# Turning q and k of each head on VectorE and by DMAs between partitions instead of on TensorE, in a two-layer trunk

## The chip, the cores and the metric

The kernel runs on one core of one Trainium2 chip. The time is device microseconds of one execution of the whole program. The engines in question are TensorE (PE in the rows; PEld are its weight loads), VectorE (DVE), ScalarE (ACT), GpSimd (POOL) and SyncE (SP); SP and POOL issue the DMAs here.

## What is computed

The program is a trunk of two layers on 512 tokens of width 2048, in f32. Each layer normalizes, scales and shifts by rows that come from a conditioning vector c, mixes the tokens, and adds the gated result to the residual. Layer 0 mixes by causal pooling, layer 1 by sparse attention with 16 heads of 128, where a small indexer picks the allowed keys of every query. Cut to what matters:

```python
def rms_norm(x, g):
    return x * lax.rsqrt(jnp.mean(x * x, axis=-1, keepdims=True) + EPS) * g

# layer 1 (dsa_branch); layer 0 is pool_branch
q, k, v, gate, qi, ki, wi = jnp.split(h @ w_in, ATTN_SPLITS, axis=-1)
q = rope_partial(q.reshape(B, L, 16, 128), positions, 32)
k = rope_partial(k.reshape(B, L, 16, 128), positions, 32)
score = einsum('bqhs,bqh->bqs', relu(einsum('bqhd,bsd->bqhs', qi, ki)), wi) * idx_scale
_, sel = lax.top_k(where(causal, score, -inf), 128)
logits = einsum('bqhd,bqkhd->bhqk', q, k[sel]) * 128 ** -0.5
o = einsum('bhqk,bqkhd->bqhd', softmax(logits), v[sel])
out = (o * silu(gate)) @ w_out
# each layer
h = rms_norm(x, norm_g[i]) * (1 + scale) + shift
x = x + gate_i * out
```

The logits contract over the head's 128 dimensions, so q and k must stand with these on the partitions, while the projection leaves them with tokens on the partitions: each needs a 512x128 transpose per head.

## The kernel before

Every f32 product is made of three matmuls on fp32r pairs: an operand is split into a high half (ScalarE, L174) and a low half, the rest (VectorE, L175), and high x high, high x low and low x high are summed. The program goes through these stages: sums of squares of x and the first norm; layer 0's projections, pooling and output; the second norm; the indexer and the choice of keys; q, k, v and the heads; layer 1's output; the final norm.

In the heads' stage the heads go in pairs j = 0..7 of an even head a and an odd head b. The projection of a pair is computed by seven products of half-size blocks, in the order P1, P5, P6, P3, P7, P2, P4. Each product has four units (kp), each unit 12 matmuls of 128x384 (q_slot, L812 to L814), into the PSUM tiles bx, by and bz. A unit's weights arrive in tiles qx or qy: one load (L734) on SP's queue, and for most products a second, accumulating load (L737) on POOL's. `q_unit` splits them into qwh and qwl three units ahead (QLOOK), four slots each; as P4's units are split, the load of the next pair's P1 goes out on SP. nb, the q, k, v of head b, is complete when P7's results are added (L951, two adds), na after P4's.

What a head then needs is a list of 13 items (head_items). They are queued in bg, and step(1) after each unit runs one of them, so the work of b stands in the program among P2, P4 and the next P1, that of a among the next pair's P1, P5, P6 and P3. The items are: rope of q and k (L541 to L544); the halves of v; `turned` for q and then for k, which makes four transposes of 128x128 into a PSUM tile (L835) and splits it into qh, ql or kh, kl; `soft` for each of four query blocks (three matmuls of 128 rows and 128 to 512 columns, L859 to L861, a masked maximum on VectorE, exp on ScalarE); norm_p; trans (transposes of the probabilities, L879); and pvs. The logits stand in tiles lg, a ring of three; the same ring serves s3_item and y_split.

A norm (norm_r) makes the reciprocal of mean square plus EPS, its root on ScalarE, and one Newton step in four GpSimd operations (L277 to L280); norm_b then turns the result into a row with TensorE (L286). At the start SP issues the row c (cr), the table of columns (cl), the first 1 MB of modulation weights (ms) for the scale, and then the 16 tiles of x; mod_scale and mod_shift are each a product of ms with silu(c), summed on VectorE (L226).

The order within an engine is settled when the program is built; at run time an instruction waits for semaphores. DMAs on SP and ACT share eight completion semaphores (DMAHW0 to 7), those on POOL eight others (DMASW0 to 7).

Of the kernel before, what the change touches and what calls it, by code (L numbers as in the profile page):

```python
# [52 lines left out]
def trunk(ctx, tc, xT, cols, crow, pos, modT, win, wgrp, wout0, widx, wgate, wqkv, wout1, out):  # L53
    nc = tc.nc
    mm = nc.tensor.matmul

    cp = ctx.enter_context(tc.tile_pool(name="cp", bufs=1))
    hp = ctx.enter_context(tc.tile_pool(name="hp", bufs=1))
    dp = ctx.enter_context(tc.tile_pool(name="dp", bufs=1, space=DRAM))
    P = {}  # L60
# [18 lines left out]
    turn = [0]  # L79
# [4 lines left out]
    def att():  # L84
        return P["ps"].tile([128, 512], F32, name="att", tag="att", bufs=P["natt"])
# [170 lines left out]
    def cond_rows(pool, rows):
        cr = rows()
        nc.sync.dma_start(cr, crow)
        cb = pool.tile([128, D], F32, name="cb")
        for q in range(4):  # L260
            p = bank()
            mm(p, ones[0:1, :], cr[:, 512 * q:512 * q + 512], start=True, stop=True)
            nc.scalar.activation(cb[:, 512 * q:512 * q + 512], p, AF.Silu)
        cell["cb"] = cb


    def norm_r(t0, t1):
        nb = (t1 - t0) // 128
        p = misc()
        for j in range(nb):  # L270
            mm(p[:, j:j + 1], P["acc"][:, t0 + j * 128:t0 + j * 128 + 128], ones[:, 0:1], start=True, stop=True)
        s = P["tp"].tile([128, 4, 4], F32, name="nrm", tag="nrm", bufs=2)
        v, r, u, iv = (s[:, a, 0:nb] for a in range(4))
        nc.vector.tensor_scalar(v, p[:, 0:nb], 1.0 / D, EPS, op0=OP.mult, op1=OP.add)
        nc.vector.reciprocal(iv, v)
        nc.scalar.activation(r, iv, AF.Sqrt)
        nc.gpsimd.tensor_tensor(u, r, r, op=OP.mult)  # L277
        nc.gpsimd.tensor_tensor(u, u, v, op=OP.mult)
        nc.gpsimd.tensor_scalar(u, u, -0.5, 1.5, op0=OP.mult, op1=OP.add)
        nc.gpsimd.tensor_tensor(r, r, u, op=OP.mult)  # L280
        return r

    def norm_b(r, t0, t1):
        p2 = misc()
        for j in range((t1 - t0) // 128):
            nc.tensor.transpose(p2[:, j * 128:j * 128 + 128], r[:, j:j + 1].to_broadcast([128, 128]), ident)  # L286
        nc.scalar.copy(P["rbc"][:, t0:t1], p2[:, 0:t1 - t0])

# [34 lines left out]
    em = ExitStack()  # L323
    ml = em.enter_context(tc.tile_pool(name="ml", bufs=1))

    cond_rows(ml, lambda: ml.tile([1, D], F32, name="cr", tag="ms", bufs=3))
    nc.sync.dma_start(cl, cols)
    for i in range(2):
        nc.vector.tensor_scalar(b1[:, i, :], mb_[:, 48 * i + 16:48 * i + 32], 1.0, None, op0=OP.add)
    mod_scale(ml, 0, 0)()  # L330
    acc2 = hp.tile([128, T], F32, name="acc2", tag="lo0")
    xs = []
    for k in range(KT):
        x_t = hp.tile([128, T], F32, name=f"x{k}", tag=f"hi{k}")
        nc.sync.dma_start(x_t, xT[k])
        add_square(x_t, 0, T, k < 2, lambda: hp.tile([128, T], F32, name=f"sq{k}", tag=f"lo{k}"),
                   to=(P["acc"], acc2)[k % 2])
        xs.append(x_t)
    nc.vector.tensor_tensor(P["acc"], P["acc"], acc2, op=OP.add)
    mod_shift(ml, 0, 0)()  # L340
    prefetch(1)
    norm_b(norm_r(0, T), 0, T)

    def mk(k):
        return lambda: (make_h(0, k, xs[k], 0, T), done.add(("h", k)))
# [187 lines left out]

    (cosa, sina), (cosi, sini) = rot["a"], rot["i"]

    def rope(pool, tag, x, cs, sn, shape, h):
        bc = lambda t: t[:, :, None, :].to_broadcast(shape[:3] + [t.shape[-1]])
        nel = shape[1] * shape[2]
        t1 = pool.tile([128, nel, 2 * h], F32, name="rt1", tag=tag + "1").rearrange("p (a b) c -> p a b c", a=shape[1])
        t2 = pool.tile([128, nel, 2 * h], F32, name="rt2", tag=tag + "2").rearrange("p (a b) c -> p a b c", a=shape[1])  # L540
        nc.vector.tensor_tensor(t1, x, bc(cs), op=OP.mult)  # L541
        nc.vector.tensor_tensor(t2[:, :, :, 0:h], x[:, :, :, h:2 * h], bc(sn[:, :, 0:h]), op=OP.mult)
        nc.vector.tensor_tensor(t2[:, :, :, h:2 * h], x[:, :, :, 0:h], bc(sn[:, :, h:2 * h]), op=OP.mult)
        nc.vector.tensor_tensor(x, t1, t2, op=OP.add)  # L544
# [24 lines left out]
    for tt, o in early:  # L569
        n = o.shape[-1]  # L570
# [20 lines left out]
    for c, tts in ((0, (2, 3)), (1, (1, 2, 3)), (2, (1, 2, 3))):  # L591
# [9 lines left out]
        else:  # L601
            a, n = ((0, 10), (10, 6))[c - 1]
# [179 lines left out]
    ap = el.enter_context(tc.tile_pool(name="ap", bufs=1, reuse_waits="tile"))  # L782
# [33 lines left out]

    def s3_item(k):
        def run():
            ha = ap.tile([128, T], F32, name="lg", tag="lg", bufs=3)
# [8 lines left out]
    def head_items(h, nat):  # L828
        x = nat.rearrange("p t (o d) -> p t o d", o=3)
        cell = {}  # L830

        def turned(s, nm):
            p = att()
            for tt in range(4):
                nc.tensor.transpose(p[:, tt * 128:tt * 128 + 128], x[:, tt, s, :], ident)  # L835
            a = ap.tile([128, T], F32R, name=nm + "h", tag=nm + "h")
            b = ap.tile([128, T], F32R, name=nm + "l", tag=nm + "l")
            split(a, b, p)
            cell[nm] = (a, b)

        def rot_qk():
            rope(ap, "rh", x[:, :, 0:2, 0:32], cosa, sina, [128, 4, 2, 32], 16)

        def keep_v():
            vh = ap.tile([128, 4, 128], F32R, name="vh", tag="vh")
# [8 lines left out]
        def soft(qb):  # L854
            n = (qb + 1) * 128
            (qh, ql), (kh, kl) = cell["q"], cell["k"]
            o = att()[:, 0:n]
            qs = slice(qb * 128, qb * 128 + 128)
            mm(o, qh[:, qs], kh[:, 0:n], start=True, stop=False)  # L859
            mm(o, qh[:, qs], kl[:, 0:n], start=False, stop=False)  # L860
            mm(o, ql[:, qs], kh[:, 0:n], start=False, stop=True)  # L861
            lg = ap.tile([128, n], F32, name="lg", tag="lg", bufs=3)
# [50 lines left out]
    def y_split(k):  # L913
        src = y[k]
        if k < HEADS - 2:
            src = ap.tile([128, T], F32, name="yr", tag="lg", bufs=3)
            nc.sync.dma_start(src, yd[k])
        yT[k] = hslots(k)
        split(yT[k][0], yT[k][1], src)

    ev = nc.vector.tensor_tensor
    for j in range(HEADS // 2):
        a, b = 2 * j, 2 * j + 1
        banks = {}
        na = nb = None
        for u in range(28):
# [4 lines left out]
            if role[prod] not in banks:  # L931
                r = role[prod]
# [46 lines left out]
    op_ = es.enter_context(tc.tile_pool(name="op", bufs=1))  # L979
# [97 lines left out]
```

## Time and profile before

| what | value |
|---|---|
| median of 3 runs | 1656.59 us (1652.77 to 1659.31) |
| the profiled execution | 1654.79 us, span 1653.0 us |
| TensorE busy | 1616.7 us, 98% of the span |
| VectorE, ScalarE, GpSimd busy | 1258.4, 726.2, 135.8 us |
| heads' stage | about 930 to 1447 us; one pair takes 70.50 us |

The span is the time from the first to the last instruction of the profiled execution; its own time is a little longer. A share is an average over stages: TensorE waits mainly in the first 32 us and the last 20.

### The profile page before, as it was taken

To read this page: it belongs to the slowest core of one execution; us is meant where nothing else is said; L and a number is where in the kernel's file an instruction comes from. 1 tells how busy PE (TensorE), PEld (TensorE's weight loads), DVE (VectorE), ACT (ScalarE), POOL (GpSimd) and SP (SyncE) were. 2 spreads that over 40 slices of the span, in tenths; PEclk is the share of its full clock that TensorE was granted. 3 is DMA by queue.
4 is the path that set the end of the run, shared out by engine and by line. 5 is a ranking of instruction groups with operands and counts; after the bars stand their busy time and mean duration, and the time that the engine had idled before them with its cause. 6 is when DMAs were issued, how large, how long until landed. Compare 5 with 4: busy or idle time off the path is not lost.

```text
span 1653.0 us, 23832 instructions
## 1 busy us (share of the span) xinstructions
PE 1616.7 (98%) x8892; PEld 1460.8 (88%) x8892; DVE 1258.4 (76%) x2132; ACT 726.2 (44%) x1149; POOL 135.8 (8%) x258
## 2 busy tenths in 40 slices
PE   4999999999999999999999999999999999999997
PEld 2888888888889999998889999999999999988897
DVE  6899998999974689865796676676776777756854
ACT  4622221334223456453324555455545555544244
POOL 1000000000000000010002121121312213000000
PEclk9999999999999999999999999999999999999999
DMA  8888888552786786443347896886968778637954
GB/s 323 326 299 310 325 337 327 223 178 101 286 300 208 233 249 187 143 143 114 102 149 169 197 174 164 185 165 177 165 170 178 171 180 162 205 109 288 364 175 166
DMA packets 105381, 348.21 MB, mean 211 GB/s; under 512 B 11825, under 2 KB 20145, under 8 KB 92849
## 3 DMA queue, kind: packets, MB, share of 16 engines
q1 hardware_dynamic: 86834, 296.35, 51.2%
q0 software_dynamic: 18432, 50.34, 18.2%
q8 instruction: 70, 1.15, 0.3%
q14 instruction: 45, 0.37, 0.1%
HBM read 330.39 MB, written 16.25 MB: 210 GB/s over the span
## 4 chain that ended last, share of the span: by engine, by line
PE 72%; issue 24%; POOL 1%; DVE 1%; DMA 1%; ACT 0%; POOLq 0%; SPq 0%; DVEq 0%; ACTq 0%
PE acc L191 8%; PE acc L192 8%; PE acc L193 8%; PE att L191 4%; PE att L192 4%; PE att L193 4%; PE by L812 4%; PE by L814 4%; PE by L813 4%; PE bz L812 2%; PE bz L814 2%; PE bx L812 2%; PE bz L813 2%; PE bx L814 2%; PE bx L813 2%
## 5 line engine op out<-in xcount | busy, mean ns | idle before, releaser
L148 ACT CAST wh<-st 128x1024 fp32r<-128x1024 f32 (+1 forms) x232 | 236.1, 1018 | 497.9 <-PE acc L192 267.3
L150 DVE TENSOR_TENSOR wl<-st,wh 128x1024 fp32r<-128x1024 f32 (+1 forms) x232 | 274.0, 1181 | 149.8 <-ACT wh L148 147.1
L192 PE MATMUL acc<-lo,wh 128*128 128x512 f32 (+1 forms) x810 | 299.7, 370 | 0.0
L191 PE MATMUL acc<-hi,wh 128*128 128x512 f32 (+1 forms) x810 | 299.6, 371 | 0.0
L193 PE MATMUL acc<-hi,wl 128*128 128x512 f32 (+1 forms) x810 | 299.2, 370 | 0.0
L226 DVE SCALAR_TENSOR_TENSOR ms<-ms,cb 128x2048 f32<-128x2048 f32 x96 | 218.9, 2285 | 17.4 <-DMA ms<-modT 8.8
L192 PEld LDWEIGHTS acc<-lo,wh 128*128 128x128 f32 x810 | 153.1, 189 | 26.4 <-DVE lo L175 0.2
L191 PEld LDWEIGHTS acc<-hi,wh 128*128 128x128 f32 x810 | 153.0, 189 | 26.5 <-ACT hi L174 0.4
L193 PEld LDWEIGHTS acc<-hi,wl 128*128 128x128 f32 x810 | 153.1, 189 | 26.2
L175 DVE TENSOR_TENSOR qwl<-qx,qwh 128x768 fp32r<-128x768 f32 x128 | 122.1, 956 | 67.1 <-ACT qwh L174 64.6
L174 ACT CAST qwh<-qx 128x768 fp32r<-128x768 f32 x128 | 106.7, 836 | 103.4 <-PE bz L814 37.3
L191 PE MATMUL att<-hi,wh 128*128 128x512 f32 (+1 forms) x406 | 148.8, 367 | 2.2 <-ACT hi L312 2.2
L192 PE MATMUL att<-lo,wh 128*128 128x512 f32 (+1 forms) x406 | 149.1, 367 | 0.0
L193 PE MATMUL att<-hi,wl 128*128 128x512 f32 (+1 forms) x406 | 148.9, 367 | 0.0
L175 DVE TENSOR_TENSOR qwl<-qy,qwh 128x768 fp32r<-128x768 f32 x96 | 91.7, 956 | 48.9 <-ACT qwh L174 47.0
L737 POOL DMA_DIRECT2D qx<-wqkv x96 | 83.3, 873 | 432.1 <-DVE stt L866 199.6
L174 ACT CAST qwh<-qy 128x768 fp32r<-128x768 f32 x96 | 80.0, 834 | 87.0 <-PE by L814 39.5
L191 PEld LDWEIGHTS att<-hi,wh 128*128 128x128 f32 x406 | 77.1, 190 | 14.9 <-ACT hi L312 2.6
L812 PE MATMUL bx<-qwh,hi 128*128 128x384 f32 x256 | 89.2, 349 | 0.0
L192 PEld LDWEIGHTS att<-lo,wh 128*128 128x128 f32 x406 | 77.1, 190 | 13.2 <-DVE lo L313 0.8
L193 PEld LDWEIGHTS att<-hi,wl 128*128 128x128 f32 x406 | 77.2, 190 | 12.5
L812 PE MATMUL by<-qwh,hi 128*128 128x384 f32 x256 | 88.2, 345 | 0.0
(286 smaller groups left out, 3507.2 us busy)
## 6 DMA issues: line engine op xcount, KB each, us to landing
ms<-modT SPq DMA_DIRECT2D x96, 1024.0 KB, 7.2
st<-wout SPq DMA_DIRECT2D x88, 512.0 KB, 4.4
qx<-wqkv POOLq DMA_DIRECT2D x96, 384.0 KB, 5.7
st<-win SPq DMA_DIRECT2D x64, 512.0 KB, 5.1
qy<-wqkv SPq DMA_DIRECT2D x64, 384.0 KB, 3.5
st<-wgate SPq DMA_DIRECT2D x40, 512.0 KB, 3.6
qx<-wqkv SPq DMA_DIRECT2D x32, 384.0 KB, 3.2
qy<-wqkv POOLq DMA_DIRECT2D x32, 384.0 KB, 5.9
```

What stands on the lines that cost most here:

```text
L148: nc.scalar.copy(wh, st)
L150: nc.vector.tensor_tensor(wl, st, wh.bitcast(F32), op=OP.subtract)
L174: nc.scalar.copy(hi, src)
L175: nc.vector.tensor_tensor(lo, src, hi.bitcast(F32), op=OP.subtract)
L191: mm(o, wh[:, kk, ms], rh[:, t0:t1], start=first, stop=False)
L192: mm(o, wh[:, kk, ms], rl[:, t0:t1], start=False, stop=False)
L193: mm(o, wl[:, kk, ms], rh[:, t0:t1], start=False, stop=last)
L226: nc.vector.scalar_tensor_tensor(st, st, 1.0, cell["cb"], op0=OP.mult, op1=OP.mult, accum_out=dst)
L737: nc.gpsimd.dma_start(d[kp], blk(j, name, kp), accum_op=OP.add)
L812: mm(o, hi, wh[:, kk, :], start=first, stop=False, skip_group_check=not opens)
L813: mm(o, hi, wl[:, kk, :], start=False, stop=False, skip_group_check=not opens)
L814: mm(o, lo, wh[:, kk, :], start=False, stop=last, skip_group_check=not opens)
```

## The change

The heads: `turn` takes the place of `turned`. Four VectorE instructions transpose every 32x32 block of a head's q (128 tokens each) into a tile b; 16 DMAs on SP's queue, each 32 partitions of 512 bytes (16 KB), then put block row i and block column j of b where they belong in a second tile f. The same is done for k in the same item. `halves`, two items later, splits f through a strided view. There are 8 VectorE instructions and 32 DMAs for a head, and no transposes on TensorE for q and k. Both tiles and rope's two temporaries stand in the lg ring, which has four slots in place of three.

The start: x is loaded right after cr, ahead of cl and ms; the norm stands ahead of the scale's product in the program; the first weights are loaded ahead of the shift's. All norms: the Newton step is three VectorE operations (refine).

```diff
-        nc.gpsimd.tensor_tensor(u, r, r, op=OP.mult)
-        nc.gpsimd.tensor_tensor(u, u, v, op=OP.mult)
-        nc.gpsimd.tensor_scalar(u, u, -0.5, 1.5, op0=OP.mult, op1=OP.add)
-        nc.gpsimd.tensor_tensor(r, r, u, op=OP.mult)
+        refine(r, u, v)
...
+    def refine(r, u, v):
+        stt = nc.vector.scalar_tensor_tensor
+        nc.vector.tensor_tensor(u, r, r, op=OP.mult)
+        stt(u, u, -0.5, v, op0=OP.mult, op1=OP.mult)
+        stt(r, u, 1.5, r, op0=OP.add, op1=OP.mult)
...
+    cr = ml.tile([1, D], F32, name="cr", tag="ms", bufs=3)
+    nc.sync.dma_start(cr, crow)
+    xs = [hp.tile([128, T], F32, name=f"x{k}", tag=f"hi{k}") for k in range(KT)]
+    for k in range(KT):
+        nc.sync.dma_start(xs[k], xT[k])
...
+    nc.vector.tensor_tensor(P["acc"], P["acc"], acc2, op=OP.add)
+    norm_b(norm_r(0, T), 0, T)
     nc.sync.dma_start(cl, cols)
...
     mod_scale(ml, 0, 0)()
...
+    prefetch(1)
     mod_shift(ml, 0, 0)()
-    prefetch(1)
-    norm_b(norm_r(0, T), 0, T)
...
-        def turned(s, nm):
-            p = att()
+        def turn(s, nm):
+            b = ap.tile([128, T], F32, name="lg", tag="lg", bufs=4)
+            f = ap.tile([128, T], F32, name="lg", tag="lg", bufs=4)
             for tt in range(4):
-                nc.tensor.transpose(p[:, tt * 128:tt * 128 + 128], x[:, tt, s, :], ident)
+                nc.vector.transpose(b.rearrange("p (j t c) -> p t j c", j=4, t=4)[:, tt],
+                                    x[:, tt, s, :].rearrange("p (j c) -> p j c", c=32))
+            for i in range(4):
+                for j in range(4):
+                    nc.sync.dma_start(f[32 * j:32 * j + 32, 128 * i:128 * i + 128],
+                                      b[32 * i:32 * i + 32, 128 * j:128 * j + 128])
+            cell[nm] = f
+
+        def halves(nm):
             a = ap.tile([128, T], F32R, name=nm + "h", tag=nm + "h")
             b = ap.tile([128, T], F32R, name=nm + "l", tag=nm + "l")
-            split(a, b, p)
+            v = lambda t: t.rearrange("p (t i c) -> p t i c", t=4, i=4)
+            split(v(a), v(b), cell[nm].rearrange("p (i t c) -> p t i c", i=4, t=4))
             cell[nm] = (a, b)
...
-        return [at((rot_qk,)), at((keep_v,)), at((turned, 0, "q")), at((turned, 1, "k")), at((soft, 0)),
+        return [at((rot_qk,)), at((turn, 0, "q"), (turn, 1, "k")), at((keep_v,)), at((halves, "q"), (halves, "k")), at((soft, 0)),
```

How the order changes is seen in three places, all at the end of the first pair. The first is SP's queue, from the last qy loads on. Before:

```order
L734 DMA qy<-wqkv 128x768 [waits DMAHW4_49,DMAHW0_49,DVE_49]
L734 DMA qx<-wqkv 128x768 [waits DMASW0_49,DVE_49]
L734 DMA qx<-wqkv 128x768 [waits DMASW1_49,DVE_49]
L734 DMA qx<-wqkv 128x768 [waits DMASW2_49,DVE_49]
L734 DMA qx<-wqkv 128x768 [waits DMASW3_49,DVE_49]
L899 DMA yd<-yg 128x512 [waits DMAHW1_49,DVE_49]
```

And of the change:

```order
L739 DMA qy<-wqkv 128x768 [waits DMAHW4_49,DMAHW0_49,DVE_49]
L847 DMA lg<-lg 32x128 [waits DVE_49]
L847 DMA lg<-lg 32x128 x3
L847 DMA lg<-lg 32x128 [waits DMAHW1_49]
L847 DMA lg<-lg 32x128 [waits DMAHW2_49]
...
L847 DMA lg<-lg 32x128 [waits DMAHW5_49,DVE_49]
...
L847 DMA lg<-lg 32x128 [waits DMAHW4_49]
L739 DMA qx<-wqkv 128x768 [waits DMAHW5_49,DMASW0_49,Activation_49]
L739 DMA qx<-wqkv 128x768 [waits DMAHW6_49,DMASW1_49,DVE_49]
```

The 32 block moves of head b (the row that also waits for DVE is k's first) stand between the last qy load and the loads of the next P1. From the fifth on each waits for the completion of an earlier one.

The second place is TensorE. Before, q's transposes stand within P2 and the logits of block 0 ahead of P4:

```order
L814 MATMUL bx<-qwh,lo_5256 128x384
L835 MATMUL att<-ident,nb 128x128 [waits DVE_49]
L835 MATMUL att<-ident,nb 128x128 x3
L812 MATMUL bx<-qwh,hi_5291 128x384 [waits Activation_49]
...
L814 MATMUL bx<-qwh,lo_5443 128x384
L859 MATMUL att<-kh,qh 128x128 [waits DVE_49,Activation_49]
L860 MATMUL att<-kl,qh 128x128 [waits DVE_49]
L861 MATMUL att<-kh,ql 128x128
L812 MATMUL by<-qwh,hi_5141 128x384
```

Of the change, where P4 ends and the next pair's P1 begins:

```order
L819 MATMUL by<-qwh,lo_5440 128x384
L876 MATMUL att<-kh,qh 128x128 [waits Activation_49]
L876 MATMUL att<-kh,qh 128x256 [waits PE_49]
L877 MATMUL att<-kl,qh 128x128 [waits DVE_49]
...
L817 MATMUL bx<-qwh,hi_4799 128x384 [waits Activation_49]
L876 MATMUL att<-kh,qh 128x384 [waits DVE_49]
L877 MATMUL att<-kl,qh 128x384
L878 MATMUL att<-kh,ql 128x384
L818 MATMUL bx<-qwl,hi_4799 128x384 [waits DVE_49]
```

All of P2 and P4 (96 matmuls) now stand in a row without a transpose or logits between them, and the four blocks of logits stand after P4 and among P1's first units. Those of head a stand a product later than before, in P3.

The third place is VectorE, from the end of b's rope to its first softmax, in the changed kernel; before, ql and kl stand among the four qwl there and wait for ScalarE alone:

```order
L175 TENSOR_TENSOR vl<-nb,vh 128x512 [waits Activation_49]
L843 STREAM_TRANSPOSE lg<-nb 128x4x32 [waits DVE_49]
L843 STREAM_TRANSPOSE lg<-nb 128x4x32 x3
L175 TENSOR_TENSOR qwl<-qx,qwh 128x768 [waits DMASW0_49,Activation_49]
L843 STREAM_TRANSPOSE lg<-nb 128x4x32 x4
L175 TENSOR_TENSOR qwl<-qx,qwh 128x768 [waits DMASW1_49,Activation_49]
L175 TENSOR_TENSOR qwl<-qx,qwh 128x768 [waits DMASW2_49,Activation_49]
L175 TENSOR_TENSOR qwl<-qx,qwh 128x768 [waits DMASW3_49,PE_49,Activation_49]
L175 TENSOR_TENSOR ql<-lg,qh 128x512 [waits DMAHW4_49,DMAHW3_49,DMAHW5_49,DMAHW2_49,DMAHW6_49,DMAHW1_49,DMAHW7_49,DMAHW0_49,Activation_49]
```

The eight block transposes stand behind v's low half, and ql and kl stand behind all of P4's weight halves and wait for all eight DMA semaphores.

## Rows read from the trace of the kernel before

**Rows 1.** The page, section 1: busy time, share of the span, instructions.

```profile
PE 1616.7 (98%) x8892; PEld 1460.8 (88%) x8892; DVE 1258.4 (76%) x2132; ACT 726.2 (44%) x1149; POOL 135.8 (8%) x258
```

**Rows 2.** Windows: length; busy us of PE, PEld, DVE, ACT, POOL; clock, DMA share, GB/s.

```profile
0.00:40.00 40.00, 18.22 (x44) 10.96 (x45) 25.72 (x38) 18.76 (x29) 6.77 (x77) 1.00 0.85 320
40.00:330.00 290.00, 290.00 (x1281) 240.27 (x1280) 275.20 (x385) 92.02 (x116) 0.00 (x0) 1.00 0.82 308
620.60:624.00 3.40, 3.39 (x29) 3.39 (x29) 1.87 (x4) 2.05 (x4) 0.00 (x0) 1.00 0.81 264
934.60:1005.10 70.50, 70.50 (x422) 68.89 (x421) 49.86 (x103) 38.61 (x67) 13.88 (x16) 1.00 0.79 173
1615.00:1617.50 2.50, 1.11 (x10) 0.92 (x9) 1.81 (x3) 0.93 (x2) 0.00 (x0) 1.00 0.70 242
1617.50:1621.00 3.50, 3.50 (x18) 3.50 (x18) 1.55 (x3) 2.53 (x3) 0.42 (x3) 0.51 0.49 149
```

**Rows 3.** Timeline of TensorE at the end of the first pair: start, us, operation.

```profile
1000.78 0.34 PE L812 MATMUL bx<-qwh,hi 128*128 128x384 f32 x1
...
1004.77 0.34 PE L814 MATMUL bx<-qwh,lo 128*128 128x384 f32 x1
...
1005.56 0.33 PE L813 MATMUL bx<-qwl,hi 128*128 128x384 f32 x1
...
1019.83 0.39 PE L859 MATMUL att<-kh,qh 128*128 128x512 f32 x1
...
1020.66 0.42 PE L812 MATMUL bx<-qwh,hi 128*128 128x384 f32 x1
```

**Rows 4.** Timeline of VectorE behind the adds of nb.

```profile
1002.23 0.28 DVE L543 TENSOR_TENSOR rt<-nb,ras 128x128 f32<-128x128 f32 x1
1002.43 0.95 DVE L175 TENSOR_TENSOR qwl<-qy,qwh 128x768 fp32r<-128x768 f32 x1
...
1003.64 0.69 DVE L175 TENSOR_TENSOR vl<-nb,vh 128x512 fp32r<-128x512 f32 x1
```

**Rows 5.** Timeline of SP at the start.

```profile
0.75 0.34 SPq L258 DMA_DIRECT2D cr<-crow  x1
1.15 0.36 SPq L327 DMA_DIRECT2D cl<-cols  x1
...
2.02 0.91 SPq L335 DMA_DIRECT2D x<-xT  x2
```

**Rows 6.** DMA issues by tile: KB each, median us from issue to landing.

```profile
qx<-wqkv SPq DMA_DIRECT2D x32, 384.0 KB, 3.2
x<-xT SPq DMA_DIRECT2D x16, 256.0 KB, 5.5
...
posi<-pos SPq DMA_DIRECT2D x1, 2.0 KB, 2.3
```

**Rows 7.** The tile kh: ns min/median/max of its halves.

```profile
L174 ACT CAST kh<-att x16: 577/582/587, 937.9 to 1466.1; 128x512 fp32r<-128x512 f32 x16
L175 DVE TENSOR_TENSOR kl<-att,kh x16: 679/683/684, 938.9 to 1467.5; 128x512 fp32r<-128x512 f32 x16
```

**Rows 8.** Timeline of SP at the end of the first pair.

```profile
1005.22 7.52 SPq L734 DMA_DIRECT2D qx<-wqkv  x4
```

**Rows 9.** The page, section 5: busy us, mean ns, idle before.

```profile
L175 DVE TENSOR_TENSOR qwl<-qx,qwh 128x768 fp32r<-128x768 f32 x128 | 122.1, 956 | 67.1 <-ACT qwh L174 64.6
L174 ACT CAST qwh<-qx 128x768 fp32r<-128x768 f32 x128 | 106.7, 836 | 103.4 <-PE bz L814 37.3
```

**Rows 10.** Timeline of TensorE at the second norm.

```profile
620.61 0.43 PE L286 MATMUL misc<-ident,nrm 128*128 128x128 f32 x2 [1.72 <-POOL nrm L280]
```

**Rows 11.** Timeline of GpSimd at the first norm.

```profile
24.68 1.91 POOL L277 TENSOR_TENSOR nrm<-nrm 128x4 f32<-128x4 f32 x1 [20.90 <-ACT nrm L276]
```

**Rows 12.** Timeline of TensorE at the first norm.

```profile
28.55 1.11 PE L286 MATMUL misc<-ident,nrm 128*128 128x128 f32 x4 [4.61 <-POOL nrm L280]
```

**Rows 13.** Timeline of VectorE at the first norm.

```profile
24.27 2.26 DVE L226 SCALAR_TENSOR_TENSOR ms<-ms,cb 128x2048 f32<-128x2048 f32 x1
```

More of the change, by code (lines that the diff above doesn't have):

```diff
@@ L254, in trunk, with cond_rows @@
     cell = {}
[L256 to L264, printed above, removed]
+    def cond_rows(pool):
+        cell["cb"] = pool.tile([128, D], F32, name="cb")
+        nc.sync.dma_start(cell["cb"], crow.to_broadcast([128, D]))
+        nc.scalar.activation(cell["cb"], cell["cb"], AF.Silu)
     def norm_r(t0, t1):
@@ L324, in trunk @@
     ml = em.enter_context(tc.tile_pool(name="ml", bufs=1))
-    cond_rows(ml, lambda: ml.tile([1, D], F32, name="cr", tag="ms", bufs=3))
+    cr = ml.tile([1, D], F32, name="cr", tag="ms", bufs=3)
+    nc.sync.dma_start(cr, crow)
+    cell["cb"] = ml.tile([128, D], F32, name="cb")
+    xs = [hp.tile([128, T], F32, name=f"x{k}", tag=f"hi{k}") for k in range(KT)]
+    for k in range(KT):
+        nc.sync.dma_start(xs[k], xT[k])
+    for q in range(4):
+        p = bank()
+        mm(p, ones[0:1, :], cr[:, 512 * q:512 * q + 512], start=True, stop=True)
+        nc.scalar.activation(cell["cb"][:, 512 * q:512 * q + 512], p, AF.Silu)
+    acc2 = hp.tile([128, T], F32, name="acc2", tag="lo0")
+    for k in range(KT):
+        add_square(xs[k], 0, T, k < 2, lambda: hp.tile([128, T], F32, name=f"sq{k}", tag=f"lo{k}"),
+                   to=(P["acc"], acc2)[k % 2])
+    nc.vector.tensor_tensor(P["acc"], P["acc"], acc2, op=OP.add)
+    norm_b(norm_r(0, T), 0, T)
     nc.sync.dma_start(cl, cols)
@@ L330, in trunk @@
     mod_scale(ml, 0, 0)()
[L331 to L339, printed above, removed]
+    prefetch(1)
     mod_shift(ml, 0, 0)()
-    prefetch(1)
-    norm_b(norm_r(0, T), 0, T)
     def mk(k):
@@ L534, in trunk, with rope @@
     (cosa, sina), (cosi, sini) = rot["a"], rot["i"]
-    def rope(pool, tag, x, cs, sn, shape, h):
+    def rope(pool, tag, x, cs, sn, shape, h, bufs=0):
         bc = lambda t: t[:, :, None, :].to_broadcast(shape[:3] + [t.shape[-1]])
         nel = shape[1] * shape[2]
-        t1 = pool.tile([128, nel, 2 * h], F32, name="rt1", tag=tag + "1").rearrange("p (a b) c -> p a b c", a=shape[1])
-        t2 = pool.tile([128, nel, 2 * h], F32, name="rt2", tag=tag + "2").rearrange("p (a b) c -> p a b c", a=shape[1])
+        tags = [dict(tag=tag, bufs=bufs)] * 2 if bufs else [dict(tag=tag + c) for c in "12"]
+        t1 = pool.tile([128, nel, 2 * h], F32, name="rt1", **tags[0]).rearrange("p (a b) c -> p a b c", a=shape[1])
+        t2 = pool.tile([128, nel, 2 * h], F32, name="rt2", **tags[1]).rearrange("p (a b) c -> p a b c", a=shape[1])
         nc.vector.tensor_tensor(t1, x, bc(cs), op=OP.mult)
@@ L818, in run @@
         def run():
-            ha = ap.tile([128, T], F32, name="lg", tag="lg", bufs=3)
+            ha = ap.tile([128, T], F32, name="lg", tag="lg", bufs=4)
             whole(ha, k)
@@ L830, in head_items @@
         cell = {}
-        def turned(s, nm):
-            p = att()
+        def turn(s, nm):
+            b = ap.tile([128, T], F32, name="lg", tag="lg", bufs=4)
+            f = ap.tile([128, T], F32, name="lg", tag="lg", bufs=4)
             for tt in range(4):
-                nc.tensor.transpose(p[:, tt * 128:tt * 128 + 128], x[:, tt, s, :], ident)
+                nc.vector.transpose(b.rearrange("p (j t c) -> p t j c", j=4, t=4)[:, tt],
[6 more added lines that the diff above has]
+        def halves(nm):
             a = ap.tile([128, T], F32R, name=nm + "h", tag=nm + "h")
             b = ap.tile([128, T], F32R, name=nm + "l", tag=nm + "l")
-            split(a, b, p)
+            v = lambda t: t.rearrange("p (t i c) -> p t i c", t=4, i=4)
+            split(v(a), v(b), cell[nm].rearrange("p (i t c) -> p t i c", i=4, t=4))
             cell[nm] = (a, b)
         def rot_qk():
-            rope(ap, "rh", x[:, :, 0:2, 0:32], cosa, sina, [128, 4, 2, 32], 16)
+            rope(ap, "lg", x[:, :, 0:2, 0:32], cosa, sina, [128, 4, 2, 32], 16, 4)
         def keep_v():
@@ L861, in soft @@
             mm(o, ql[:, qs], kh[:, 0:n], start=False, stop=True)
-            lg = ap.tile([128, n], F32, name="lg", tag="lg", bufs=3)
+            lg = ap.tile([128, n], F32, name="lg", tag="lg", bufs=4)
             st = ap.tile([128, 4], F32, name="stt", tag="stt", bufs=6)
@@ L915, in y_split @@
         if k < HEADS - 2:
-            src = ap.tile([128, T], F32, name="yr", tag="lg", bufs=3)
+            src = ap.tile([128, T], F32, name="yr", tag="lg", bufs=4)
             nc.sync.dma_start(src, yd[k])
@@ L983, in keep1 @@
         return x2[mt][:, t0:t1]
-    cell["cb"] = op_.tile([128, D], F32, name="cb")
-    nc.sync.dma_start(cell["cb"], crow.to_broadcast([128, D]))
-    nc.scalar.activation(cell["cb"], cell["cb"], AF.Silu)
+    cond_rows(op_)
     for k in range(4):
```

## Prediction

> **What bounds the kernel now.** The first thing to read is the busy table: TensorE works in 98% of the span [rows 1], so an edit pays only by what it takes off TensorE or by what it makes TensorE wait. The windows come next [rows 2]: from 40 to 330 us TensorE is busy in all 290.00 us, so a start that is shorter moves everything behind it forward; and in one period of a pair of heads (934.60 to 1005.10, 70.50 us) it is busy in all 70.50 us while VectorE has 49.86 and ScalarE 38.61. The stage of the heads therefore has no slack on TensorE, and about 20 us of a period are free on VectorE. What TensorE does at the end of a pair stands in its timeline [rows 3]: P2 begins at 1000.78, a group of four transposes stands behind the matmul of 1004.77, the last softmax block of head b begins at 1019.83, and the next pair's P1 at 1020.66. Head b's q, k, v are complete only as P2 begins, so all that lies between rope and the first logits of b has to fit under P2 and P4.
>
> **What is removed.** From 1004.77 to 1005.56 lie two steps of ordinary matmuls and one group of four transposes: 0.79 us. Ordinary matmuls start 0.1735 us apart (1000.78 to 1004.77 holds 23), two are 0.347, so a group costs 0.445 us. A head has two groups, for q and for k: 16 heads have 32, 14.3 us, 0.89 per head.
>
> **What is added, head b.** VectorE ends rope and starts v's low half at 1003.64 (0.69 us); the block transposes follow. No row shows one. The nearest is a 128x128 multiply of f32, 0.28 us and 0.20 to the next start [rows 4]; four are 0.8 to 1.1 us, and q's blocks can go out at about 1005.3. The Trainium skill (VectorE: DVE Perf Modes, The three transpose paths) speaks against the change at this point: VectorE turns 32x32 blocks only, which leaves the grid of blocks to be moved, and the page's rules advise TensorE for 128x128. By that advice the 14.3 us stay on TensorE and nothing of the following is paid; no row of before shows VectorE's form.
>
> Moving the blocks is 32 DMAs for a head, all on SP's queue, 16 KB each. SP's first issues start at 0.75, 1.15 and 2.02 (with one between the last two), and two loads of x take 0.91 [rows 5]: 0.40 to 0.46 apart. Size hardly enters: cr, one row of 8 KB, took 0.34 and cl, 128 rows, 0.36. An issue with nothing behind it cannot be under 0.33 by these; I take 0.40 apart, with 0.38 and 0.475 as ends. A DMA of 2 KB took 2.3 us to land, one of 384 KB 3.2 [rows 6]; I take 2.3 for 16 KB. There are eight completion semaphores, so each DMA waits for the landing of the one eight earlier: 8 x 0.40 = 3.2 us is more than 2.3, so that wait costs nothing at 2.3. Then k's last block lands at 1005.3 + 31 x 0.40 + 2.3 = 1020.0. ScalarE's high half takes 0.58 and VectorE's low half 0.68 [rows 7]: the first logits can start at 1020.6, all three matmuls at 1021.3.
>
> TensorE reaches that place earlier than before: by the order shown, P2 and P4 run their 96 matmuls without anything between, 1000.78 + 96 x 0.1735 = 1017.4. It stands still for 3.2 us (2.3 to 5.7 with the ends).
>
> Behind the 32 blocks on SP stand the first weights of the next pair's P1. Before, their issue began at 1005.22 [rows 8]; now at 1005.3 + 32 x 0.40 = 1018.1. They land 3.2 later [rows 6] and need 0.84 on ScalarE and 0.96 on VectorE [rows 9]: 1018.1 + 3.2 + 0.84 + 0.96 = 1023.1 for P1's second matmul. The softmax of the first three blocks and one matmul of P1 fit in front of it. Left to do at 1023.1, and done before 1020.66 in the kernel before, are the fourth block and three transposes of logits, less P1's one matmul: the fourth block and two transposes are the 0.83 us from 1019.83 to 1020.66 [rows 3], the third transpose and the matmul about cancel. That is 1023.1 + 0.83 - 1020.66 = 3.3 us per pair, with the saved transposes of b already in it. To this I add 1.2 us (0 to 1.5): four blocks of softmax, spread over P4's four units before, now stand with P1's weight halves on VectorE and ScalarE within two units. And 0.5 us (0 to 1.7) for the clock: from 1615.00 to 1617.50 TensorE stood still for 1.4 of 2.5 us, and in the 3.5 us after it the granted clock was 0.51, the lower level of 1.2 GHz [rows 2], which costs 3.5 x 0.49 = 1.7 us. A wait of 1.72 us before 620.61 [rows 10] was followed by 3.4 us at 1.00, the level of 2.4 GHz [rows 2]. So a halt may cost this or nothing, and I take about a third. Together 5.0 us per pair.
>
> **Head a.** Its q, k, v are complete after P4 and its first logits now stand in P3, behind P5, P6 and 13 matmuls of P3: rope and the transposes stand at P5's start, so about 109 x 0.1735 = 19 us cover them, against 32 x 0.40 + 2.3 + 1.3 = 16.4 us. It gains the 0.89 us; I take half of it off, for blocks that queue behind other loads on SP: -0.44 (-0.89 to +2).
>
> **Start.** Before, x is loaded behind cl and 1 MB of ms, after, ahead of them. At the 320 GB/s of the first 40 us [rows 2] that is 3.3 us. POOL's four steps begin at 24.68 [rows 11], and TensorE's next work at 28.55 waits for them [rows 12]. On VectorE they become three small operations of about 0.2 us, but a product of ms (24.27, 2.26 us [rows 13]) stands ahead of them in its order and ends at 26.5, so only about 1.4 of the 3.9 us comes back. The second ms, which the first activations also need, is loaded behind as many bytes as before and one block of weights more. I take -3.3 (0 to -4.7, the sum of both).
>
> **Other Newton steps.** At 620.61 TensorE had waited 1.72 us for POOL's last one [rows 10]; three other norms have the same steps beside other work. I take -1.5 in all (0 to -3, nearly two waits of this size).
>
> **Sum.** 8 pairs x 5.0 (the last has no P1 to stand behind but has its softmax exposed, I count it like the others) = 40.0; 8 heads a x -0.44 = -3.5; start -3.3; Newton -1.5: +31.7 us. The profiled run took 1654.8, so 1686.5; the median of the three runs lies 1.8 above it: 1688.
>
> **Rivals.**
> Faster: the blocks arrive in time. Then nothing waits, and 14.3 + 3.3 + 1.5 = 19.1 us are saved: 1637. It needs k's high half by 1017.4 and P1's weights by 1019.8, where TensorE is without b's transposes; the first asks for issues at most (1017.4 - 0.58 - 2.3 - 1005.3) / 31 = 0.297 us apart. For it: 512 KB per head are 1.6 us at 320 GB/s, and short issues may overlap. Against it: no issue of SP in the trace is under 0.33. The Trainium skill states the premise of this rival (DMA: Bandwidth & Descriptors, Issuing engines are not separate DMA queues): the time a sequencer spends to start a DMA is usually small beside the DMA. For blocks of 16 KB the trace does not agree: 0.33 us of issue for 0.05 us of data at 320 GB/s.
>
> About the same: TensorE waits, but 0.38 apart and with neither crowding nor a slower clock. P1's second matmul is then at 1022.3 at the latest, 2.4 us per pair: 19.2 - 7.1 - 4.8 = +7, 1664; with a start that gives back all of its bound it comes within 8 us of before.
>
> Much slower: the landing of a block is not 2.3 but 5 us. For it: the loads of x, 256 KB each and issued one upon another, took 5.5 [rows 6], and in the heads' stage the blocks run beside accumulating weight loads. Against it: x waited for its own bytes, and a block is a sixteenth of one. Eight in flight per 5 us give 0.63 us per block; 32 take 20 us, P1's weights are issued at 1025.3 and ready at 1030.3, which is 10.5 us per pair in place of 3.3; with heads a, whose 16.4 us of need become 26 against 19 of cover, up to +100 us. Between that and the forecast lie 1720 to 1755. It decides from a landing of 3.2 us on.
>
> The change does not do what it says: the scheduler could put TensorE's work between P2, P4 and the logits otherwise; the order shown excludes it.
>
> **How the numbers follow.** Less than 0.5% (8 us) can hardly be told from no change in this kernel, whose three runs lie 6.5 us apart. Chances: a stall of 3 to 8 us per pair 0.66, much slower 0.12, about the same 0.11, faster 0.11. The predicted time is the first case's, 1688. Its own range is 1668 (2.5 us per pair) to 1715 (8 us per pair). The range for 8 in 10 takes in the upper part of the same-case and the lower part of the much slower one: 1656 to 1722. Faster by over 0.5%: 0.11; within 0.5%: 0.11; slower: 0.78.
>
> **What would show it.** Right: at the end of each pair TensorE idles about 3 us before the first logits of b, released by ScalarE's kh; SP shows 32 issues about 0.4 us apart; P1's weights are issued after 1017; a period is about 75 us instead of 70.5; the first matmul of a gemm comes some 3 us sooner; VectorE's Newton steps take 0.2 us each. Wrong: no idle time before the logits (issues faster than 0.30 apart), or issues more than 0.5 apart (waits on landings), or stalls at head a's logits in P3.

## The result, and the profile after

The changed kernel takes 1854.78 us (median of 4 runs, 1851.82 to 1858.04) against 1655.51 us of the kernel before beside it: a ratio of 1.1206, 95% interval 1.1186 to 1.1227. Slower was forecast, but 1688 us, in a range to 1722: the loss is six times as large.

The page's busy table, which answers to [rows 1], shows that TensorE is no longer always at work:

```profile
PE 1658.4 (89%) x8764; PEld 1484.8 (80%) x8764; DVE 1280.6 (69%) x2275; ACT 724.1 (39%) x1150; POOL 126.4 (7%) x238
```

It has 128 matmuls less and 42 us more of busy time. The windows (length; busy us of the five engines; granted clock, DMA share, GB/s) answer to [rows 2]:

```profile
40.00:330.00 290.00, 290.00 (x1281) 240.14 (x1280) 275.30 (x386) 91.95 (x116) 0.00 (x0) 1.00 0.82 305
1052.41:1149.49 97.08, 74.48 (x404) 70.69 (x404) 52.29 (x119) 36.62 (x66) 13.78 (x16) 0.89 0.61 136
1041.95:1052.41 10.46, 0.00 (x0) 0.00 (x0) 1.64 (x4) 0.90 (x2) 0.00 (x0) 0.74 0.19 51
1052.41:1057.00 4.59, 4.41 (x14) 3.89 (x15) 3.33 (x10) 2.06 (x4) 0.84 (x1) 0.50 0.77 276
1100.94:1105.00 4.06, 4.06 (x15) 4.06 (x16) 2.56 (x8) 1.67 (x5) 0.00 (x0) 0.50 0.30 100
```

A pair takes 97.08 us instead of 70.50. TensorE is idle in 97.08 - 74.48 = 22.6 us of it. Of its 74.48 us of work some 68.7 would be needed (70.50 without 1.78 of transposes): the other 5.8 us are mostly the slower clock behind the halts. The last three rows show it: a halt of head b, 10.46 us without one matmul, then 4.59 us at a granted clock of 0.50, the level of 1.2 GHz, and the same for 4.06 us behind a's halt. Half of these 8.65 us, 4.3, is lost by the clock; the remaining 1.5 was not followed further. So 26.6 = 22.6 + 5.8 - 1.8.

TensorE's timeline shows two halts, in brackets idle time and releaser: that of b which ends at the head of this period, and a's within it (at the period's end stands the next one of b, 10.21 us):

```profile
1052.41 0.48 PE L876 MATMUL att<-kh,qh 128*128 128x128 f32 x1 [10.46 <-ACT kh L174]
```

```profile
1100.94 0.47 PE L876 MATMUL att<-kh,qh 128*128 128x128 f32 x1 [10.85 <-ACT kh L174]
```

Both end with kh, which waits for blocks. Over the eight pairs b's halts are 10.2 to 12.1 us, a's 4.1 to 10.9 (the one shown is the longest; their mean is 7.1), 144.3 us in all. SP's timeline over the same pair answers to [rows 8]:

```profile
1029.61 20.61 SPq L847 DMA_DIRECT2D lg<-lg  x32
1050.34 1.94 SPq L739 DMA_DIRECT2D qx<-wqkv  x4
1070.47 2.43 SPq L847 DMA_DIRECT2D lg<-lg  x4
1073.00 0.53 SPq L916 DMA_DIRECT2D yd<-yg  x1
1073.58 20.71 SPq L847 DMA_DIRECT2D lg<-lg  x28
1094.34 0.83 SPq L869 DMA_DIRECT2D yg<-yd  x1
```

b's 32 issues take 20.61 us, 0.64 each; P4's last matmul starts at 1041.61, when the queue is at block 19. The instructions of the DMAs' line (ns min/median/max) and the time to landing say where that comes from:

```profile
L847 SPq DMA_DIRECT2D lg<-lg x512: 507/589/1857, 932.1 to 1675.7; - x171
...
DMA to landing us min/median/max: 1.7/1.8/7.4
```

The landing is quick, 1.8 us in the median, as it is in each of b's series; a's blocks take longer, as shown below. No DMA waits for the one eight earlier. The issue itself is long: 0.589 us, and some 0.045 to the next.

The start gained less than the norm did. Before, TensorE made the norm's row at 28.55 and the first product at 31.88; after (timeline of TensorE, the first row from before):

```profile
31.88 1.22 PE L191 MATMUL att<-hi,wh 128*128 128x512 f32 x2 [2.22 <-ACT hi L312]
```

```profile
23.71 1.09 PE L285 MATMUL misc<-ident,nrm 128*128 128x128 f32 x4 [3.27 <-DVE nrm L280]
29.48 1.22 PE L191 MATMUL att<-hi,wh 128*128 128x512 f32 x2 [4.68 <-ACT hi L311]
```

The norm is 4.8 us earlier, the first product 2.4: it now waits for the activation hi, which needs the second product of ms (VectorE, 26.12 to 28.41). With all Newton steps the heads' stage begins 5.1 us earlier (first matmul of P1 at 883.5 instead of 888.6).

### The profile page after: what moved, and what is told of

It is laid out like the page before. It is cut to its first block, busy times and chain, and to the rows that moved or that the text cites. A ratio compares the mean times of both kernels' runs of the same rounds, so it can differ in the third digit from the quotient of the medians.

```text
span 1856.3 us, 24496 instructions
## 1 busy us (share of the span) xinstructions
PE 1658.4 (89%) x8764; PEld 1484.8 (80%) x8764; DVE 1280.6 (69%) x2275; ACT 724.1 (39%) x1150; POOL 126.4 (7%) x238
## 4 chain that ended last, share of the span: by engine, by line
PE 58%; SPq 16%; DMA 9%; DVE 9%; issue 5%; ACT 2%; POOL 1%; ACTq 0%; POOLq 0%; DVEq 0%
SPq L847 15%; PE acc L191 9%; PE acc L193 9%; PE acc L192 9%; PE att L193 6%; PE att L192 6%; PE att L191 6%; DMA qx<-wqkv 3%; DMA lg<-lg 3%; DVE qwl L175 2%; DVE score L671 1%; PE bz L818 1%; PE bz L819 1%; DVE wl L150 1%; PE bz L817 1%
## 5 line engine op out<-in xcount | busy, mean ns | idle before, releaser
L876 PE MATMUL att<-kh,qh 128*128 128x128 f32 (+1 forms) x64 | 29.1, 508 | 146.0 <-ACT kh L174 144.3
L876 PEld LDWEIGHTS att<-kh,qh 128*128 128x128 f32 x64 | 16.6, 292 | 152.9 <-ACT kh L174 150.0
L175 DVE TENSOR_TENSOR kl<-lg,kh 128x512 fp32r<-128x512 f32 x16 | 11.1, 692 | 125.5 <-ACT kh L174 116.7
```

## The experiments

Twelve kernels ran. The issue time was the first theory, the landing behind other loads the rival, and the place at which the logits stand in TensorE's order a third. This place isn't the same in all of these kernels: in the changed kernel b's first logits stand behind P4 and a's 13 matmuls into P3 (22 in the first pair); where another kernel differs, it is said.

**TensorE's transposes put back.** The start, the Newton steps and the ring of four stay.

```diff
-at((rot_qk,)), at((turn, 0, "q"), (turn, 1, "k")), at((keep_v,)), at((halves, "q"), (halves, "k")),
+at((rot_qk,)), at((keep_v,)), at((turned, 0, "q")), at((turned, 1, "k")),
```

> The changed kernel with q and k turned by TensorE again; the start, the Newton steps and the ring of four stay changed. If all of the loss is in the block moves, this stands below before by what the start shows (its first gemm matmul at 29.5 instead of 31.9 us) and a little for the Newton steps: 1651 to 1654 us. If the start or the ring costs something later, it is at or above 1656.

1649.4 us against 1656.57: a ratio of 0.9959 (0.9946 to 0.9971). It is below both kernels, a little below my 1651 to 1654 too, and the version to keep. All of the loss, and 7 us more, is in the turning of q and k.

**The moves left out.**

```diff
-            for i in range(4):
-                for j in range(4):
-                    nc.sync.dma_start(f[32 * j:32 * j + 32, 128 * i:128 * i + 128],
-                                      b[32 * i:32 * i + 32, 128 * j:128 * j + 128])
-            cell[nm] = f
+            cell[nm] = b
```

> VectorE's block transposes stay, the 32 DMAs per head are left out, and the halves are taken from the unmoved blocks (so the logits are not the reference's). Theory of the issue time (the 32 issues 0.63 us apart are what TensorE waits for): no halt, 16 x 0.89 us of transposes saved, 1636 to 1642 us. Rival (VectorE's transposes and the softmax gathered behind P4 cost time by themselves): 1660 us or more.

1638.15 us, 0.9893 (0.9878 to 0.9909), without a halt for the halves over 0.8 us. The block transposes themselves cost nothing that can be seen; the DMAs cost all of it. Against the 1649.4 us with TensorE's transposes it is 11 us less: so much could be had at most if the moves were free.

**What an issue costs.** Series of DMAs that nothing waits for, in six heads of the kernel with TensorE's transposes; one series as an example:

```diff
+            for i in range(8):
+                nc.sync.dma_start(b[r:r + 32, c], a[0:32, 0:128])
```

> The kernel with TensorE's transposes and, in six heads, a series of 4 or 8 DMAs on SP that nothing waits for: 32 rows of 512 bytes from SBUF to other partitions of SBUF, 128 rows of 512 bytes SBUF to SBUF, 32 rows from DRAM to SBUF, 32 rows from SBUF to DRAM, 128 rows from DRAM to SBUF, 32 rows within the same partitions. If the issue costs 0.59 us because both ends lie in SBUF, the first, second and last are at 0.5 to 0.6 us and the others at 0.33 to 0.40. If it is the 32 rows, the first, third, fourth and last are. If it is only that they follow closely, all are. If it is the move between partitions, only the first is (and the last is short).

The instructions of each series (ns min/median/max), in the order of the expectation:

```profile
L862 SPq DMA_DIRECT2D lg<-lg x8: 513/582/605, 1054.3 to 1059.9; - x8
```

```profile
L864 SPq DMA_DIRECT2D lg<-lg x4: 465/564/601, 1124.3 to 1127.0; - x4
```

```profile
L866 SPq DMA_DIRECT2D lg<-pd x8: 318/420/508, 1192.6 to 1199.3; - x8
```

```profile
L868 SPq DMA_DIRECT2D pe<-lg x8: 412/421/449, 1265.3 to 1269.8; - x8
```

```profile
L870 SPq DMA_DIRECT2D lg<-pd x4: 319/444/472, 1333.6 to 1338.4; - x4
```

```profile
L872 SPq DMA_DIRECT2D lg<-lg x8: 507/584/591, 1406.3 to 1411.7; - x8
```

Both ends in SBUF: 0.56 to 0.58 us, with 32 rows or 128, to other partitions or not. One end in DRAM: 0.42 to 0.44, where the DMA of 32 rows and that of 128 again agree. With both ends in SBUF this is as expected, with one in DRAM 0.02 to 0.04 us above my 0.33 to 0.40. The shortest of a series, behind a pause or a load of weights, is 0.07 to 0.13 us under the median (0.01 from SBUF to DRAM). So in these series it is the kind of its ends, and next to it the close succession, that make the issue long, and no size. That isn't the whole rule: a load of weights right behind eight moves within SBUF took 0.51 us (at 1060.59) and one among them, after a pause, 0.34 (at 1055.55), and the reads of the next experiment, with one end in DRAM but their pieces of 512 bytes apart there, took 0.51 in the median. Why an issue takes longer stays open.

**The blocks through DRAM,** 10 DMAs a head instead of 32.

```diff
+            nc.sync.dma_start(d.rearrange("i p j c -> (i p) (j c)"), b)
+            for i in range(4):
+                nc.sync.dma_start(f[:, 128 * i:128 * i + 128], d[i].rearrange("p j c -> j p c"))
```

> The blocks go through DRAM: one DMA of 128 partitions out and four of 128 partitions back for q, as many for k, 10 issues per head instead of 32. Theory of the issue time: 10 x 0.4 us and two landings of 2 to 3 us are 8 to 10 us, which P2 and P4 cover (12 us); P1's weights are issued some 4 us after the transposes. 1636 to 1650 us. Rival (it is the landing of small pieces, not the issues; the pieces of 512 bytes are as many as before, and there is one landing more): halts of 5 us or more stay, over 1700 us.

A miss: 1825.64 us, 1.1017 (1.1001 to 1.1033), and by number what the rival has. SP's timeline at a's moves of the first pair shows that it issues little and waits much:

```profile
968.41 0.33 SPq L846 DMA_DIRECT2D td<-lg  x1
968.99 0.33 SPq L916 DMA_DIRECT2D yd<-yg  x1
973.82 2.53 SPq L848 DMA_DIRECT2D lg<-td  x4
976.39 0.77 SPq L846 DMA_DIRECT2D td<-lg  x1
977.20 0.47 SPq L869 DMA_DIRECT2D yg<-yd  x1
984.54 2.17 SPq L848 DMA_DIRECT2D lg<-td  x4
```

The reads by themselves (ns min/median/max):

```profile
L848 SPq DMA_DIRECT2D lg<-td x128: 499/514/742, 934.7 to 1636.2; - x128
```

The reads follow their writes 5.4 and 8.2 us later: that is a landing, not 2.3 us. TensorE waited 4.3 to 6.7 us for b, whose logits stand 3 matmuls into the next P1 here, and 13.1 to 14.3 us for a (3.3 in the last pair), whose logits stand 15 to 25 matmuls into P6, earlier than in the changed kernel. Few issues are not enough where landings come in a row beside other loads. Whether small pieces land later than large ones isn't shown by it.

**The accumulating loads left out** (the products are made of the first loads alone).

```diff
     def more(d, kp, j, name):
-        nc.gpsimd.dma_start(d[kp], blk(j, name, kp), accum_op=OP.add)
+        pass
```

> The changed kernel without the accumulating weight loads on POOL's queue (the products are then made from the first loads alone). Theory of the issue time: b's halts of 10 to 12 us stay, since no accumulating load runs beside b's blocks; a's halts, where the last blocks landed 5 to 7 us after their issue, fall from 6 to 10 us to 3 or less: 1780 to 1810 us. Rival (the accumulating loads are behind both halts): b's halts fall too, under 1720 us. Rival (they are behind neither): 1840 us or more.

1803.24 us, 1.0901 (1.0882 to 1.0919), as the issue time has it for b: b halts 9.9 to 12.2 us as before, a 3.4 to 4.6 (I had 3 or less) instead of 4.1 to 10.9. The DMA issues by tile (KB each, us to landing) at the end of a's blocks, first of the changed kernel (1088 to 1102 us, the second pair, where they land latest), then of this one (990 to 999 us, the first pair):

```profile
qy<-wqkv POOLq DMA_DIRECT2D x4, 384.0 KB, 7.4
yg<-yd SPq DMA_DIRECT2D x1, 256.0 KB, 7.7
lg<-lg SPq DMA_DIRECT2D x8, 16.0 KB, 5.1
```

```profile
qy<-wqkv SPq DMA_DIRECT2D x1, 384.0 KB, 3.4
yg<-yd SPq DMA_DIRECT2D x1, 256.0 KB, 3.1
lg<-lg SPq DMA_DIRECT2D x11, 16.0 KB, 1.8
```

Beside accumulating loads a block lands in 5.1 us, without them in 1.8. Over all 32 blocks of a the median is 3.6 to 5.1 us in the first seven pairs of the changed kernel, 1.75 in the last, which has no such loads beside it, and 1.8 in every pair here. So b's halt is the issue time alone; a's has both in it: a mean of 7.1 us with these loads, 4.0 without. Their bytes went with them, so this doesn't tell whether it is the accumulating that holds the blocks back or any load of that size. The changed kernel's page (queue: packets, MB, share of the 16 engines' time) shows that their queue, the software one, takes about twice the engines' time per MB:

```profile
q1 hardware_dynamic: 111410, 304.77, 47.5%
q0 software_dynamic: 18432, 50.34, 15.5%
```

**Only q on VectorE,** 16 DMAs a head.

```diff
+at((rot_qk,)), at((turn, 0, "q")), at((keep_v,)), at((halves, "q"), (turned, 1, "k")), at((soft, 0)),
```

> Only q is turned by VectorE and moved by 16 DMAs, k by TensorE. Theory of the issue time: 16 issues 0.635 us apart end 10.2 us after their start and land 1.8 us later, which P2 and P4 (11.9 us from the start of the issues) just cover: b halts by 0 to 2 us instead of 10.5, a not at all; 8 x 0.445 us of transposes a pair are saved half: 1646 to 1665 us. Rival (what a block waits for is its landing behind the accumulating loads of POOL, however few they are): a's halts of 5 us or more stay and the time is 1690 or more.

1753.88 us, 1.0596 (1.0581 to 1.0612). b is as the issue time has it (halts of 1.6 to 3.3 us instead of 10 to 12, with the logits 35 matmuls into P4, 2.3 us earlier). a (6.4 to 8.1 us, 0.2 in the last pair) and the time are where the rival has them. But a's logits stand 12 matmuls into P6 here, 49 matmuls or 8.5 us earlier than in the changed kernel, so these halts come of the place and of the landings (a median of 5.1 to 5.4 us) together; this run doesn't part them. My forecast had left out both.

**k's DMAs on ScalarE's queue.**

```diff
+            q = nc.sync if s == 0 else nc.scalar
```

> The 16 DMAs of k go out on ScalarE's queue, those of q stay on SP's. Theory of the issue time: each queue needs 16 x 0.635 = 10.2 us, b's halts fall from 10.5 to 2 us or less; ScalarE loses 10 us per head of issuing and is late with some weight halves: 1660 to 1720 us. Rival (the 512 moves of 16 KB are bound by the DMA engines or by landings, not by the issuing engine): no shorter than 1830 us.

1792.05 us, 1.0833 (1.0805 to 1.0860). The time is in neither range. TensorE's waits for kh fall from 144 to 3 us, as the issue time has it, and another wait comes up ahead of them: 94.8 us for P4's and P6's weight halves, which stand behind these issues on ScalarE. Its timeline, and the instructions of the two queues (ns min/median/max):

```profile
934.00 11.87 ACTq L848 DMA_DIRECT2D lg<-lg  x16
945.99 0.83 ACT L174 CAST qwh<-qx 128x768 fp32r<-128x768 f32 x1 [13.51 <-DMA lg<-lg]
```

```profile
L848 SPq DMA_DIRECT2D lg<-lg x256: 507/590/1600, 932.4 to 1597.9; - x128
L848 ACTq DMA_DIRECT2D lg<-lg x256: 514/601/1906, 934.0 to 1598.8; - x128
```

An issue took 0.60 us there, as on SP; the 11.87 us of this series are more than 16 of them because one took 1.9. Both queues kept their pace at the same time, so the pace is that of the issuing queue and not of the DMA engines behind both.

**12 DMAs a head:** q and k in one tile, the four diagonal blocks copied by ScalarE.

```diff
+                    to, fr = f[32 * j:32 * j + 32, 256 * i:256 * i + 256], b[32 * i:32 * i + 32, 256 * j:256 * j + 256]
+                    if i == j:
+                        nc.scalar.copy(to, fr)
+                    else:
+                        nc.sync.dma_start(to, fr)
```

The four slots of lg become two tiles of twice the width here, in the next kernel and in the last one of this section; what this alone costs was not run.

> q and k of a head stand in one tile, so that one DMA moves both of a block (32 rows of 1 KB), and the four diagonal blocks, which don't change partition, are copied by ScalarE: 12 issues per head instead of 32, all bytes as before. Theory of the issue time: 12 x 0.635 = 7.6 us and a landing of 1.8 are within P2 and P4, so b doesn't halt, a little at a at most; 1638 to 1648 us, that is, below the kernel with TensorE's transposes (1649.4). Rival (bytes or number of pieces moved): halts stay, 1750 us or more.

1739.44 us, 1.0506 (1.0481 to 1.0531), and again the time of neither. b's 12 issues of the first pair took 8.28 us. But in this order the logits of b stand 33 matmuls into P4 and those of a 12 matmuls into P6, earlier than in the changed kernel: the program's order follows an expected landing, and the chip's is later. Halts of 1.0 to 2.7 us at b, 2.7 to 7.1 at a.

**The same, with the logits later.**

```diff
+        late = [at()] * (2 if h % 2 else 4)
+        return [at((rot_qk,), (turn,)), at((keep_v,)), *late, at((halves, 0, "q"), (halves, 1, "k")), at((soft, 0)),
```

> pairs12 with the halves and the logits standing later in the program: behind P6 for a (36 matmuls, 6.2 us later), for b almost where they were. Theory of the place: with 12 DMAs the blocks are there by then, a's halts of 4 to 7 us go to 0 to 1.5 us, b's of 1 to 2.5 stay: 1739 - 8 x 7 = 1683, 1668 to 1700 us. Rival (the halt follows the landing wherever the logits stand, since loads push it): 1720 or more.

1712.80 us, 1.0345 (1.0317 to 1.0373), between the two ranges. TensorE no longer waits for a's kh (all such waits are 12.3 us, b's, instead of 58.2), as the place has it; but of these 46 us the time gained only 27. The landing is as late as before (13 to 16 us behind the first issue in both), and a part of the wait came back by ScalarE, whose order has the last weight half of P6 behind a's qh (timelines of ScalarE and TensorE in the fourth pair):

```profile
1211.65 0.62 ACT L174 CAST qh<-f 128x512 fp32r<-128x512 f32 x1 [8.79 <-DMA f<-b]
1212.18 0.82 ACT L174 CAST qwh<-qx 128x768 fp32r<-128x768 f32 x1
```

```profile
1213.06 0.44 PE L819 MATMUL by<-qwh,s2h 128*128 128x384 f32 x1 [2.75 <-ACT qwh L174]
```

TensorE waits 14.0 and 3.7 us for these weight halves, and 9.0 us for the halves of the probabilities, since the softmax now falls into P3 beside the weights. So the rival has a point too: the landing is waited for, if not at the logits.

**One half of the heads each.** The change for b alone, then for a alone, the others by TensorE:

```diff
+        if h % 2 == 0:
+            return [at((rot_qk,)), at((keep_v,)), at((turned, 0, "q")), at((turned, 1, "k")), at((soft, 0)),
```

> The change for odd heads (b) alone, 32 DMAs a head as in the changed kernel; even heads (a) are turned by TensorE. If b's halts are the issue time and nothing of a's, b halts 10 to 12 us in each pair and the slower clock behind it costs 3 to 5: 1649.4 - 7 + 8 x 15 = 1762, 1745 to 1780 us. Rival (b's halt comes from a's blocks and loads pushing it): b's halts shrink under 6 us, below 1710.

1767.10 us, 1.0671 (1.0650 to 1.0691), as forecast, with b's halts at 9.9 to 11.2 us and 13.6 in the last pair.

> The change for even heads (a) alone. a's logits stand 36 matmuls into P6 in this order, about 24 us behind rope; 32 issues take 20.3 us and start late in P1, and the last landings took 5 to 7 us beside the accumulating loads. So a halts 8 to 16 us a pair, with the clock 1740 to 1800 us. Rival (a only waits because b's halt shifts it): a halts 3 us or less, under 1680.

1731.39 us, 1.0447 (1.0423 to 1.0470), below the forecast's range: a halts 3.9 to 9.4 us. Against 1649.4 the two are +117.7 and +82.0 us, together +199.7; the whole change is +205.4. Each halt arises by itself, and the two add up. That the sum is this close is in part chance, since a's logits stand 38 matmuls into P6 in this kernel, 23 earlier than in the changed one.

**b with 12 DMAs and its logits behind P4, a by TensorE.**

```diff
+        late = [at()] * (5 if h % 2 else 0)
```

> Odd heads with 12 DMAs, halves and logits behind all of P4; even heads by TensorE. The blocks of b land about 942.5 in the first pair and P4 ends at 944: no halt over 0.5 us, half of TensorE's transposes saved (7 us): 1640 to 1646 us, below both kernels and below 1649.4. Rival (VectorE's longer queue or P1's weights behind 12 issues cost a wait elsewhere): 1650 or more.

1687.69 us, 1.0186 (1.0159 to 1.0213). No halt of over 0.5 us for b's halves, but the rival is right: b's softmax falls beside P1's weight halves, and TensorE waits for its probabilities (14.6 and 7.4 us in the stage) and for those halves. None of the forms with DMAs is below the kernel before.

## Why the prediction was wrong

- **What bounds the kernel, what is removed.** Right: with the moves left out, the time falls by 11 us below the kernel with TensorE's transposes (14.3 forecast; 14.6 between the two profiled executions).
- **VectorE's block transposes.** Right: four took 0.88 to 0.89 us (0.8 to 1.1 forecast), in the changed kernel's timeline:

```profile
1028.65 0.89 DVE L843 STREAM_TRANSPOSE lg<-nb 128x128 f32<-128x128 f32 x4
1030.30 0.88 DVE L843 STREAM_TRANSPOSE lg<-nb 128x128 f32<-128x128 f32 x4
```

- **"I take 0.40 apart, with 0.38 and 0.475 as ends": the step that failed first.** It came out as 0.635. The rows behind it [rows 5] were DMAs with one end in DRAM, few of them in a row; the blocks have both ends in SBUF, and no row of before shows such a DMA. "Size hardly enters" was right; that the ends of a DMA don't enter either was taken for granted, and was not. 32 issues take 20.3 instead of 12.8 us, and b's halt is 10 to 12 us, not 3.2: most of b's 14.7 us a pair (117.7 / 8). (By its own two ends the forecast's halt is 2.6 to 5.5 us, not 2.3 to 5.7, and P1's second matmul at 0.38 apart stands at 1022.5, not 1022.3; neither matters.) Issues more than 0.5 apart were named as a sign of being wrong, but as waits for landings; there were none of these.
- **"Head a: -0.44": the step that failed next.** In the pair shown, the worst one, the cover of 19 us was right (1070.47 to TensorE's arrival at 1090.1), the need was not: 29.8 us from the first block to the start of kh at 1100.27, instead of 15.1 (the 16.4 less 1.3 for the halves). The last issue ends after 23.8 us: 20.3 at the usual pace, the rest for the store of yd that stands among them and a few longer issues. From there to kh it is another 6.0 us, the last landings, for which I had 2.3. With a alone on VectorE it costs 10.2 us a pair (82.0 / 8) instead of gaining 0.4.
- **The rival "much slower".** It had 20 us for 32 blocks, 0.63 us each, almost what was measured, but by luck: by eight landings of 5 us in flight, while b's blocks landed in 1.8 us and it was the issue that took the time. For a the late landings did come. Its +100 us, and so its range of 1720 to 1755, doesn't follow from its own terms: 8 x 10.5 for b and 8 x 7 for a are 140 us, about 1790.
- **The clock.** Forecast as 0.5 us a pair, it was about 4.3: behind each of the two halts of the period shown stand 4 to 5 us at a granted clock of 0.50.
- **P1's weights behind the blocks.** Right in mechanism (issued from 1050.34, after P4), but not what ended last: the logits of b, released by kh, were later than this or level with it.
- **Start and Newton steps.** -3.3 and -1.5 forecast. The start is -2.4, and the second product of ms takes half of the norm's gain back. For the Newton steps the rest of the 5.1 us up to the heads' stage is left, -2.7; in the profiled execution with TensorE's transposes put back the stage begins only 3.6 us earlier (885.1), so they are known no better than as -1.2 to -2.7.
- **The sum.** 31.7 forecast. By the traces: -5.1 before the stage, +183.4 in it (first to last matmul of the products, 739.0 instead of 555.5 us), +24.9 behind it, where the last pair's halts of 12.05 and 4.14 us lie: 203.2 us between the two spans.

The Trainium skill (DMA: Bandwidth & Descriptors, Issuing engines are not separate DMA queues) says that starting DMAs on several engines saves only the sequencer's time for starting them, which is usually small beside the DMA. Here that time is what TensorE waited for, 0.59 us for 16 KB with 1.8 us from issue to landing; on two engines it was saved, but ScalarE's own work then stood behind its issues.

## What to carry to other kernels

Price many small DMAs by the issue, taken from a row with the same kinds of ends and pieces and in the same close succession; if there is none, the range must be wide there, and a series that nothing waits for measures it in one run. A move that must land before TensorE's next work is judged by its whole way (issues, what stands among them on the queue, the landing beside other loads), and here a halt of some 10 us cost about a fifth more behind it through the clock (4.3 us for two). Moving the logits later in the order takes the wait off TensorE only if no other engine has to wait for the landing in its place. TensorE did the work in 0.9 us a head without a wait, and none of the forms tried here, each of which came back to it through a queue, was faster.

## What was not expected of the hardware

- A DMA from SBUF to SBUF occupied SP for 0.589 us, one with an end in DRAM for 0.42 in a series and 0.33 alone, 0.51 where its pieces lay apart in DRAM. ScalarE took 0.60 for the first kind, at the same time as SP its 0.59.
- With the accumulating loads on GpSimd's queue blocks of 16 KB landed in 5.1 us, and in 1.8 without them; whether by their accumulating or by their bytes isn't shown.
